# Three unused tiles that shift the operands of TensorE to multiples of 128 bytes

## The chip, the cores and the metric

One NeuronCore of a Trainium2 chip runs the whole program. The metric is the device time of one execution in microseconds, lower is better. The time before is the median of three executions.

## What is computed

A two-layer encoder trunk on one sequence of 1024 tokens with 1024 channels, all in float32. Cut to what matters here:

```python
for i in range(2):
    hdn = modulate(rmsnorm(x, mix_norm_g[i]), shift, scale)
    if i == 0:   # conv branch (width 31) beside a gMLP branch, one output projection
        y = conv_gmlp_mixer(hdn, ...)
    else:        # 8 heads, two softmax maps per head, relative position bias
        y = diff_attention(hdn, ...)
    x = x + gate * y
    hdn = modulate(rmsnorm(x, mlp_norm_g[i]), shift, scale)
    x = x + gate * (square(relu(hdn @ mlp_w1[i])) @ mlp_w2[i])   # 1024 -> 4096 -> 1024
return rmsnorm(x, final_norm_g)
```

## The kernel before

Activations lie transposed, channels on the 128 partitions and tokens along the free dimension, as tiles of 128 x 512 (`C = 512`, two column halves). Each float32 product is made as three matmuls in the `float32r` type (`mm3`, L124 to L128): both operands are split into a high part and the rest (`split`, L254 to L256: ScalarE casts the high part, VectorE subtracts), and high x high, high x low and low x high are summed in one bank of PSUM. In each, the weights (`whi`, `wlo`, 128 x 128) are the operand that is loaded into the array, and the activation (128 x 512) is the moving one. Weights come from memory as 128 x 1024 float32 (`raw`).

The stages in order: the first norm, the input projections, the convolution on VectorE (20 taps, L596), ScalarE and GpSimd, the gating and the output projection (to about 376 us); the first MLP (to about 1010 us); attention (to about 1690 us); the second MLP (to the end). The mixer's and the projections' moving operands are `hh`, `hl`, `zh`, `zl`, `th`, `tl`, `oh`, `ol` in pool `hp`; attention reads `K` (moving) with `Q` as weights (L957, L958), turns the softmax output `L` with transposes (L983) and reads `AT` (moving) with `Vh`, `Vl` as weights (L994 to L996).

`mlp` (L660) runs 8 groups of 7 steps. A step is one block product of a scheme of seven products with sums and differences of blocks (`UP`, `DOWN`, L656). It takes 48 matmuls: two halves of weights (`left`, L682) by four pieces of activation (`right`, L698) by two outputs by three. The activation pieces are tiles `b` of 128 x 2 x 512, high part and rest side by side, eight buffers. They are made one step ahead, or fetched from memory where an earlier group has already made them. Results leave PSUM by ScalarE and VectorE (`up_done`, L730; `down_done`, L741: VectorE L744). The modulation vectors of later layers are computed on VectorE in the background (L143).

Tiles are allocated in pools. Pools on the left side lie one behind the other from the low addresses up, those opened with `side="right"` from the top down; a pool takes the place of one that was closed before. The size of each tile is rounded up to 32 bytes. Addresses below are bytes within each partition. A 128 x 512 float32 tile takes 2048 bytes of each partition.

| tiles | pool, side | first address before | remainder to 128 | to 512 |
|---|---|---|---|---|
| `raw` (not the MLP's), `whi`, `wlo` | wp, left | 3968, 16256, 28544 | 0 | 384 |
| `h` tiles (`hh`, `hl`, `zh`, `zl`, `th`, `tl`, `f`) | hp, left | 40832 | 0 | 384 |
| `sq`, `ss`, `ht`, `ln`, `r` | tmp, left | 106368 | 0 | 384 |
| scalars of softmax and norm | small, left | 126848 | 0 | 384 |
| `b` (MLP); `K`, `V` (attention); `a0`, `a1` (conv) | mlp, at, mix, left | 127808 | 64 | 320 |
| `Q`; `raw` of the MLP | at, mlp, left | 160576 | 64 | 320 |
| `L`, `AT` | atr, right | 196576, 212960 | 96 | 480 |
| `x` | xp, right | 184288 | 96 | 480 |

`const` begins at 1152; its last tiles are `eps_r` (3840), `eps_l` (3872), `nlam` and `subg`. `wp`, `hp`, `tmp` and `small` follow it, and the pools of the stages (mix, mlp, at) begin where `small` ends, at 127808. The right side ends at 229344. The left pool `at` ends at 181056 and the right pool `atr` begins at 181216, 160 bytes above.

```python
    one = tmp.tile([P, P], F32, name="one", tag="sq", bufs=2)          # L73
    eps_r = const.tile([P, 1], F32, name="eps_r")                      # L77
    eps_l = const.tile([P, 1], F32, name="eps_l")                      # L78
```

## Time and profile before

| | |
|---|---|
| time, median of 3 (lowest to highest) | 2344.11 us (2333.05 to 2344.76) |
| the profiled execution's own time | 2343.52 us |
| its span, first to last instruction | 2341.7 us |
| granted TensorE clock, mean of the run | 0.984 of full |
| TensorE, VectorE, ScalarE, GpSimd busy | 2220.4, 1870.4, 1180.0, 238.2 us |
| matmuls | 10144 |

All instruction times are from the profiled execution. Matmuls are pipelined: the next one starts before the one in front is shown as ended, so the pace of a dense run is the difference of start times divided by the number of steps between them, not the duration of one.

### The profile page before, as it was taken

To read this page: it belongs to the slowest core of one execution; us is meant where nothing else is said; L and a number is where in the kernel's file an instruction comes from. 1 tells how busy PE (TensorE), PEld (TensorE's weight loads), DVE (VectorE), ACT (ScalarE), POOL (GpSimd) and SP (SyncE) were. 2 spreads that over 40 slices of the span, in tenths; PEclk is the share of its full clock that TensorE was granted. 3 is DMA by queue.
4 is the path that set the end of the run, shared out by engine and by line. 5 is a ranking of instruction groups with operands and counts; after the bars stand their busy time and mean duration, and the time that the engine had idled before them with its cause. 6 is when DMAs were issued, how large, how long until landed. Compare 5 with 4: busy or idle time off the path is not lost. (4 is left out here: it accounts for less than half of the span.)

```text
span 2341.7 us, 27508 instructions
## 1 busy us (share of the span) xinstructions
PE 2220.4 (95%) x10144; PEld 1798.3 (77%) x10144; DVE 1870.4 (80%) x2582; ACT 1180.0 (50%) x1753; POOL 238.2 (10%) x126
## 2 busy tenths in 40 slices
PE   4997599999999999979999999999999999999998
PEld 3786387778888888858888888887778888888886
DVE  8899899996785976986878888885798658577487
ACT  4563247633534535455656666653465354353455
POOL 0484000000000000031111111111000000000002
PEclk9998799999999999999999999999999999999999
DMA  8221553847457266233445333361362451633612
GB/s 315 84 79 45 197 183 115 305 128 276 153 178 277 86 220 245 86 110 96 86 97 107 75 83 71 86 193 60 132 238 83 162 207 54 219 123 116 237 43 73
DMA packets 113863, 335.17 MB, mean 143 GB/s; under 512 B 20576, under 2 KB 23520, under 8 KB 112704
## 3 DMA queue, kind: packets, MB, share of 16 engines
q1 hardware_dynamic: 113728, 333.41, 43.9%
q8 instruction: 80, 1.31, 0.2%
q14 instruction: 55, 0.45, 0.1%
HBM read 279.79 MB, written 53.58 MB: 142 GB/s over the span
## 5 line engine op out<-in xcount | busy, mean ns | idle before, releaser
L127 PE MATMUL ps<-b,whi 128*128 128x512 f32 (+1 forms) x1808 | 710.9, 394 | 6.5 <-DVE b L256 6.5
L126 PE MATMUL ps<-b,whi 128*128 128x512 f32 (+1 forms) x1808 | 702.2, 395 | 4.8 <-ACT b L255 3.0
L128 PE MATMUL ps<-b,wlo 128*128 128x512 f32 (+1 forms) x1808 | 703.2, 394 | 0.8 <-DVE wlo L256 0.8
L255 ACT CAST whi<-raw 128x1024 fp32r<-128x1024 f32 (+1 forms) x225 | 235.7, 1047 | 374.3 <-PE ps L127 336.9
L127 PEld LDWEIGHTS ps<-b,whi 128*128 128x128 f32 x1808 | 340.3, 188 | 90.6 <-DVE b L256 9.9
L126 PEld LDWEIGHTS ps<-b,whi 128*128 128x128 f32 x1808 | 340.0, 188 | 87.7 <-ACT b L255 3.9
L128 PEld LDWEIGHTS ps<-b,wlo 128*128 128x128 f32 x1808 | 340.1, 188 | 81.9 <-DVE wlo L256 1.6
L256 DVE TENSOR_TENSOR wlo<-raw,whi 128x1024 fp32r<-128x1024 f32 x224 | 273.3, 1220 | 146.0 <-ACT whi L255 144.0
L126 PE MATMUL ps<-hh,whi 128*128 128x512 f32 x576 | 225.4, 404 | 40.7 <-ACT hh L250 23.5
L127 PE MATMUL ps<-hl,whi 128*128 128x512 f32 x576 | 229.7, 399 | 4.3 <-DVE hl L251 2.9
L128 PE MATMUL ps<-hh,wlo 128*128 128x512 f32 x576 | 227.6, 396 | 0.0
L109 POOL TENSOR_TENSOR wlo<-raw,whi 128x1024 fp32r<-128x1024 f32 x32 | 83.5, 2612 | 1205.1 <-ACT whi L108 1044.0
L744 DVE SCALAR_TENSOR_TENSOR x<-ps,mod,x 128x512 f32<-128x512 f32 x220 | 160.3, 746 | 53.3 <-PE ps L128 53.3
L963 ACT ACTIVATE L<-L,mn 128x1024 f32<-128x1024 f32 x128 | 147.1, 1150 | 90.1 <-DVE mn L961 88.8
L961 DVE CUSTOM_DVE_ANT_0 L<-S,B 128x1024 f32<-128x1024 f32 x128 | 155.9, 1223 | 37.3 <-PE pt L983 18.4
L126 PEld LDWEIGHTS ps<-hh,whi 128*128 128x128 f32 x576 | 109.7, 191 | 68.8 <-ACT hh L250 27.7
L255 ACT CAST b<-f 128x512 fp32r<-128x512 f32 x192 | 118.0, 618 | 83.7 <-PE ps L128 83.3
L256 DVE TENSOR_TENSOR b<-f,b 128x512 fp32r<-128x512 f32 x192 | 128.9, 684 | 14.2 <-ACT b L255 14.2
L127 PEld LDWEIGHTS ps<-hl,whi 128*128 128x128 f32 x576 | 110.5, 192 | 29.4 <-DVE hl L251 5.5
L128 PEld LDWEIGHTS ps<-hh,wlo 128*128 128x128 f32 x576 | 110.5, 192 | 24.4 <-issue 0.5
L143 DVE CUSTOM_DVE_ANT_0 mraw<-mraw,cact 128x1024 f32<-128x1024 f32 x96 | 116.2, 1217 | 6.4 <-DMA mraw<-in_modw 6.3
L733 ACT COPY f<-ps 128x512 f32<-128x512 f32 x96 | 56.1, 588 | 128.4 <-PE ps L128 128.4
(201 smaller groups left out, 3473.9 us busy)
## 6 DMA issues: line engine op xcount, KB each, us to landing
b<-tspl SPq DMA_DIRECT2D x168, 512.0 KB, 5.2
raw<-in_wm SPq DMA_DIRECT2D x128, 512.0 KB, 4.6
mraw<-in_modw SPq DMA_DIRECT2D x96, 512.0 KB, 4.6
tspl<-b SPq DMA_DIRECT2D x56, 512.0 KB, 4.7
raw<-in_wqkv SPq DMA_DIRECT2D x24, 512.0 KB, 4.9
raw<-in_wo SPq DMA_DIRECT2D x17, 512.0 KB, 3.6
x<-in_xT SPq DMA_DIRECT2D x32, 256.0 KB, 5.8
tsr<-tsp SPq DMA_DIRECT2D x8, 1024.0 KB, 7.5
```

The lines of the kernel that those rows point to most:

```text
L109: (eng or dve).tensor_tensor(out=lo, in0=raw, in1=f32(hi), op=ALU.subtract)
L126: pe.matmul(ps, wh, ah, start=first, stop=False, skip_group_check=resumed)
L127: pe.matmul(ps, wh, al, start=False, stop=False, skip_group_check=resumed)
L128: newest[0] = pe.matmul(ps, wl, ah, start=False, stop=last, skip_group_check=resumed)
L143: i = dve.tensor_tensor_reduce(out=raw, in0=raw, in1=cact, op0=ALU.mult, op1=ALU.add, scale=1.0, scalar=0.0, accum_out=acc)
L255: act.copy(out=out_h, in_=src)
L256: (lo_eng or dve).tensor_tensor(out=out_l, in0=src, in1=f32(out_h), op=ALU.subtract)
L733: act.copy(out={"X1": c11, "Y1": c22, "X2": c12}[p], in_=ps)
L744: dve.scalar_tensor_tensor(out=x[m][c], in0=ps, scalar=gate(d, m), in1=x[m][c], op0=ALU.mult, op1=ALU.add)
L961: dve.tensor_tensor_reduce(out=L, in0=S, in1=win, op0=ALU.add, op1=ALU.min, scale=1.0, scalar=3e38, accum_out=mn)
L963: act.activation(out=L, in_=L, func=AF.Exp, bias=mn, scale=-1.0, accum_out=s[:, j:j + 1])
```

## The change

Three tiles are allocated that no instruction reads or writes, and the two constants of the norms share one tile of two columns.

```diff
     ones_r = const.tile([P, P], F32R, name="ones_r")
+
+    const.tile([P, 8], F32, name="fill")
+    small.tile([P, 16], F32, name="fills", tag="fills", bufs=1)
+    ctx.enter_context(tc.tile_pool(name="fillr", bufs=1, side="right")).tile([P, 24], F32, name="fillr")
     one = tmp.tile([P, P], F32, name="one", tag="sq", bufs=2)
...
-    eps_r = const.tile([P, 1], F32, name="eps_r")
-    eps_l = const.tile([P, 1], F32, name="eps_l")
+    eps = const.tile([P, 2], F32, name="eps")
+    eps_r, eps_l = eps[:, 0:1], eps[:, 1:2]
     pool.memset(eps_r, RMS_EPS)
     pool.memset(eps_l, LN_EPS)
```

By the sizes: `const` gains 32 bytes (`fill`) and loses 32 (two tiles of 4 bytes took 64, one of 8 takes 32), so `wp`, `hp` and `tmp` stay where they are. `small` grows by 64 bytes, so the left pools of the stages begin at 127872, which is 999 x 128 (remainder to 512: 384). `fillr` takes 96 bytes at the top of the right side, so all right tiles move down by 96; the side then ends at 229248, which is 1791 x 128 (remainder to 512: 384). `at` ends at 181120, and `atr` begins there. The scalar tiles in `small` move by 64 bytes.

## Rows read from the trace of the kernel before

**Rows 1.** Page: totals by engine; VectorE busy and granted clock in 40 slices.

```profile
PE 2220.4 (95%) x10144; PEld 1798.3 (77%) x10144; DVE 1870.4 (80%) x2582; ACT 1180.0 (50%) x1753; POOL 238.2 (10%) x126
...
DVE  8899899996785976986878888885798658577487
...
PEclk9998799999999999999999999999999999999999
```

**Rows 2.** Stretches: length, busy (count) by engine, clock, DMA share, GB/s; last two TensorE alone.

```profile
110.00:150.00 40.00, 40.00 (x178) 33.14 (x177) 38.90 (x32) 22.69 (x23) 29.86 (x12) 1.00 0.24 73
302.00:330.00 28.00, 28.00 (x125) 23.20 (x124) 28.00 (x48) 11.91 (x15) 0.00 (x0) 1.00 0.54 169
...
520.00:1010.00 490.00, 490.00 (x2102) 1.00 0.54 188
...
1740.00:2300.00 560.00, 560.00 (x2402) 1.00 0.41 141
```

**Rows 3.** Timeline of TensorE in the first MLP: start, length, line, operation, tiles.

```profile
599.71 0.40 PE L126 MATMUL ps<-b,whi 128*128 128x512 f32 x1
...
601.58 0.40 PE L128 MATMUL ps<-b,wlo 128*128 128x512 f32 x1
```

**Rows 4.** Timeline of TensorE in two projections of the mixer, ends of eight steps each.

```profile
119.74 0.39 PE L128 MATMUL ps<-hh,wlo 128*128 128x512 f32 x1
...
121.55 0.39 PE L127 MATMUL ps<-hl,whi 128*128 128x512 f32 x1
...
319.84 0.39 PE L128 MATMUL ps<-zh,wlo 128*128 128x512 f32 x1
...
321.65 0.39 PE L127 MATMUL ps<-zl,whi 128*128 128x512 f32 x1
```

**Rows 5.** Timeline of TensorE in attention: seven steps, four steps, transposes, 21 steps.

```profile
1105.18 0.39 PE L128 MATMUL ps<-hh,wlo 128*128 128x512 f32 x1
...
1106.77 0.39 PE L126 MATMUL ps<-hh,whi 128*128 128x512 f32 x1
...
1229.79 0.40 PE L958 MATMUL S<-K,Q 128*128 128x512 f32 x1
...
1230.71 0.40 PE L958 MATMUL S<-K,Q 128*128 128x512 f32 x1
1230.95 1.03 PE L983 MATMUL pt<-ident,L 128*128 128x128 f32 x8
...
1239.83 0.28 PE L996 MATMUL ps<-AT,Vl 128*128 128x256 f32 x1
...
1242.32 0.29 PE L996 MATMUL ps<-AT,Vl 128*128 128x256 f32 x1
```

**Rows 6.** Groups by shape, one of three lines: busy, mean ns, idle before, releasers.

```profile
L127 PE MATMUL ps<-b,whi 128*128 128x512 f32 x1776 | 701.8, 396 | 6.5 <-DVE b L256 6.5
```

**Rows 7.** The convolution's tap line: least/median/most ns, first and last start.

```profile
L596 DVE SCALAR_TENSOR_TENSOR ca<-ap,vec,ca x76: 1251/1290/1292, 86.1 to 267.7; 128x1024 f32<-128x1024 f32 x76
```

**Rows 8.** Stretches as in rows 2 before 520 us; TensorE's longest waits, 340 to 520.

```profile
400.00:430.00 30.00, 25.93 (x108) 19.43 (x107) 30.00 (x42) 18.60 (x31) 0.00 (x0) 1.00 0.66 230
...
495.00:520.00 25.00, 24.92 (x107) 20.13 (x108) 25.00 (x38) 9.64 (x14) 0.00 (x0) 1.00 0.49 151
...
PE ps L127 <- DVE b L256: 3.1, 2, 1.6
```

**Rows 9.** Timeline: VectorE reads a bank, TensorE writes the next product into it.

```profile
540.88 0.75 DVE L744 SCALAR_TENSOR_TENSOR x<-ps,mod,x 128x512 f32<-128x512 f32 x1
...
544.41 0.63 PE L126 MATMUL ps<-b,whi 128*128 128x512 f32 x2
```

**Rows 10.** TensorE's waits, whole run: total us, times, longest us.

```profile
PE ps L608 <- DVE a L597: 23.3, 1, 23.3
```

**Rows 11.** GpSimd's timeline at the start; first reader of the constants, first and last start.

```profile
0.91 0.10 POOL L80 MEMSET eps_l<- 128x1 f32 x1
...
L203 ACT ACTIVATE ln<-ps,eps_r x9: 687/687/689, 16.7 to 2312.7; 128x512 f32<-128x512 f32 x9
```

## The prediction

> **What bounds the kernel now.** I read the page's totals first, then busy time by stretch, then the timeline of single matmuls. TensorE is busy for 95% of the span at a granted clock of 0.984 over the run, and only the two slices from 176 to 293 us stand under nine tenths of full clock [rows 1]. Two stretches carry the case, one in each MLP: 520 to 1010 us and 1740 to 2300 us. In both TensorE has no gap at all, 490.00 of 490.00 and 560.00 of 560.00 us, and full clock [rows 2]. So there the time is the number of matmuls times their pace, and the question is the pace. A duration column doesn't give it, because matmuls overlap: each is shown as 0.39 us long while a new one starts every 0.23 us. The pace is the difference of starts.

> With `b` as moving operand (64 bytes past a multiple of 128), eight starts lie 601.58 - 599.71 = 1.87 us apart, 233.8 ns each [rows 3]. The long stretch agrees: 2102 matmuls touch 490.00 us, about two of them cut by its edges, so 490.00/2100 = 233.3 ns [rows 2]. I use 233.4. With operands at a multiple of 128 the same arithmetic gives 121.55 - 119.74 = 1.81 us for eight, 226.3 ns (`hh`, `hl`); 321.65 - 319.84, again 226.3 ns (`zh`, `zl`) [rows 4]; and 1106.77 - 1105.18 = 1.59 us for seven, 227.1 ns (`hh`, `hl` beside attention) [rows 5]. I use 226.7. The difference is 6.7 ns, 2.9% of a matmul.

> Is it the address, or the stage? Three things speak for the address. In attention `K`, at 64 past, takes 1230.71 - 1229.79 = 0.92 us for four, 230.0 ns, where the aligned `hh` of the same stage takes 227.1 [rows 5]. The aligned pace held while VectorE was busy for 38.90 and GpSimd for 29.86 of 40 us (40/176 = 227 ns), and, at 302 to 330 us, with VectorE never idle and DMA at 0.54, the share of the first MLP stretch (28/123 = 228 ns) [rows 2]. And the weights `whi`, `wlo` are at multiples of 128 in both cases, so the moving operand is what differs.

> **The change, part by part.** It removes and adds no matmul, copy or DMA; it moves addresses. After it `b`, `K`, `Q`, `V`, `AT`, `E`, `x` start at multiples of 128, and even the remainder to 512 becomes 384, the one that `h`, `whi` and `wlo` have now.

> (1) `b` in the gapless stretches. 1776 matmuls of 512 columns on each of three lines make 5328 [rows 6]; 2102 + 2402, less four at the edges, say 4500, are in the two stretches [rows 2]. 4500 x 6.7 ns = 30.2 us. This gain is kept only if the operands are ready 2.9% sooner. The tightest cover that I found there is a bank: VectorE ends its read at 540.88 + 0.75 = 541.63 us and TensorE writes into it again at 544.41 [rows 9], 2.8 us of slack; a step of 48 matmuls shrinks by 48 x 6.7 ns = 0.3 us. So VectorE isn't late next, unless it falls behind over some nine steps on end.

> (2) `b` before 520 us. From 400 to 430 us VectorE is busy for 30.00 of 30 us and TensorE for 25.93; TensorE waits for `b` [rows 8]. What a matmul gives up there is waited for. After 495 us TensorE is nearly gapless, 107 matmuls [rows 8]: 107 x 6.7 ns = 0.7 us. The bounds are 0 and the whole start of the MLP, 5328 - 4500 less about 220 after 1690 us, some 600 matmuls or 4.0 us; VectorE's full load puts the value near the lower end. The start of the second MLP, 1690 to 1740, has the same form: 0, at most 1.2 us.

> (3) The end, 2300 to 2342 us: some 30 whole `b`, 30 x 6.7 ns = 0.2 us, and the 96 of 256 columns of the last step, 0 to 0.5 us by the bounds of part (4). I take 0.6; bounds 0.2 and 0.7.

> (4) Attention. `K` as moving operand: 64 blocks, two maps, four matmuls each, 512 x (230.0 - 227.1) = 1.5 us. `AT` (96 past, 256 columns): 32 pairs of blocks of 24, pace (1242.32 - 1239.83)/21 = 118.6 ns [rows 5]. No aligned 256-column matmul is in the trace. Bounds: no gain, 118.6, since a weight load of 128 columns goes with each; and half of 226.7, 113.4, which is still above the pace of the transposes with the same weight load, 0.76/7 = 109 ns [rows 5]. That is 0 to 768 x 5.2 = 4.0 us. I take the middle, 2.0, as neither row is nearer. Counts are from the code (eight heads, eight blocks of queries). Softmax has its own chain over VectorE and ScalarE between two uses of TensorE, which may eat part of this, so of 3.5 us I count 3; bounds 0 and 5.5.

> (5) VectorE, ScalarE and DMA at new addresses: 0. The convolution's 76 tap instructions read the same tile at 20 offsets, 4 bytes apart, and take 1251/1290/1292 ns at least, median and most [rows 7]: no price by address. If this cover were gone, one part in a hundred of VectorE's 1870 us would be 19 us, but mostly beside TensorE.

> (6) One `eps` tile for two: the memsets stay. If readers of the first half now wait for both, they wait until 1.01 us [rows 11], while the first reader on ScalarE starts at 16.7 us [rows 11] and TensorE's sum of squares comes before it. 0. The three fillers have no instructions.

> Sum: 30.2 + 0.7 + 0 + 0.6 + 3 = 34.5 us. The profiled execution took 2343.5 us (span 2341.7 and 1.8 around it), 0.6 under the median of three, 2344.1. 2343.5 - 34.5 = 2309.0 us; against the median 2309.6. I predict 2309.

> [...] The rows show 233.4 against 226.7 ns for operands whose addresses are all multiples of 32 bytes [rows 3, 4]. [...]

> **The rivals.** A: the address costs nothing, and the 6.7 ns belong to something else of the `b` stages (two halves in one tile, the order of the banks), or the addresses don't come out as meant. Then nothing changes: 2344 us. For it: no `b` at a multiple of 128 is in the trace. Against it: `K` and `hh` in one stage. B: the pace falls, but VectorE, busy for five to nine tenths in the slices of the first gapless stretch [rows 1], becomes the bound in bursts and half of part (1) is waited for: 2309 + 15 = 2324 us. Against it: 2.8 us of slack at the tightest place. C, the other side: in 376 to 520 us TensorE's waits for VectorE grow, and the clock falls to its half level. There are about 600 `b` before 520 us; 600 x 227 ns more is 136 us, and 2309 + 136 = 2445 us. It decides when a pause is as long as those beside the low slices: TensorE waited 23.3 us for the convolution [rows 10], while the longest wait for `b` from 340 to 520 us is 1.6 us [rows 8]. Part (2) adds at most 4 us over many waits, so this is far off.

> **How the numbers follow.** Forecast 0.80, A 0.12, B 0.06, C 0.02. The low end takes all upper bounds: 30.2 + 4.0 + 1.2 + 0.7 + 5.5 = 41.6, 2302; the runs before reach 11 us under their median, and I allow 7 of it: 2295. The high end takes in B and some scatter: 2328. A measurement of this kernel tells about 0.5% (12 us) from no change, so faster is everything under 2332: forecast and B, 0.86; same is A, 0.12; slower is C, 0.02.

> **What would show it.** In the profile after: 520 to 1000 us should hold about 227 ns a `b`, so some 2115 instead of 2058 in 480 us; `K` should go to 227 ns; TensorE's gaps before 500 us should grow by 2 to 4 us; the taps should stay at 1290 ns. I'm wrong if `b` stays at 233 ns (A), if gaps appear in the two stretches (B), or if PEclk falls before 520 us (C).

## The result and the profile after

| | before | after |
|---|---|---|
| time, median | 2344.44 us (6 runs) | 2315.12 us (6 runs, 2312.81 to 2317.42) |
| ratio, 95% interval | 1 | 0.9882 [0.9862, 0.9901] |
| the profiled execution's own time | 2343.52 us | 2312.99 us |
| its span | 2341.7 us | 2311.2 us |

The kernel is 1.2% faster, 29 us by the medians. The forecast was 2309, with 2295 to 2328 as range. Four lines come in ahead of L73, so every line number behind them is four higher (L127 is L131).

The page after, totals by engine, granted clock in 40 slices, and the second of the three product lines (busy, mean ns of one | idle before it, releaser):

```profile
PE 2188.4 (95%) x10144; PEld 1800.3 (78%) x10144; DVE 1867.0 (81%) x2582; ACT 1180.8 (51%) x1753; POOL 238.5 (10%) x126
...
PEclk9998799999999999989999999999999999999999
...
L131 PE MATMUL ps<-b,whi 128*128 128x512 f32 (+1 forms) x1808 | 701.4, 389 | 6.7 <-DVE b L260 6.7
```

The same instructions run. TensorE is busy 32 us less than in [rows 1], and every other engine as long as it was. The idle time ahead of the `b` products is 6.7 us, where [rows 6] has 6.5: the gain was not turned into waits.

Stretches after, columns as in rows 2; the last two are from the view of TensorE alone:

```profile
400.00:430.00 30.00, 26.37 (x107) 20.27 (x106) 30.00 (x42) 18.50 (x30) 0.00 (x0) 0.94 0.65 228
495.00:520.00 25.00, 25.00 (x111) 20.70 (x111) 25.00 (x37) 10.36 (x15) 0.00 (x0) 1.00 0.49 151
...
520.00:1000.00 480.00, 480.00 (x2116) 1.00 0.56 194
1740.00:2280.00 540.00, 540.00 (x2396) 1.00 0.40 136
```

The MLP stretches are still without a gap, and hold more matmuls: 2116 touch the first, where 2115 were forecast. The timeline of TensorE after, 12 steps apart:

```profile
599.17 0.39 PE L130 MATMUL ps<-b,whi 128*128 128x512 f32 x1
...
601.89 0.39 PE L130 MATMUL ps<-b,whi 128*128 128x512 f32 x1
```

2.72/12 = 226.7 ns, where [rows 3] gives 233.8. From 400 to 430 us VectorE is still busy for all 30 us and the count of matmuls is the old one [rows 8].

Attention after, timeline of TensorE: three steps of `K`, then 21 of `AT`:

```profile
1237.08 0.39 PE L962 MATMUL S<-K,Q 128*128 128x512 f32 x1
...
1237.77 0.29 PE L999 MATMUL ps<-AT,Vh 128*128 128x256 f32 x1
1237.90 0.28 PE L1000 MATMUL ps<-AT,Vl 128*128 128x256 f32 x1
...
1240.41 0.28 PE L1000 MATMUL ps<-AT,Vl 128*128 128x256 f32 x1
```

`K` takes (1237.77 - 1237.08)/3 = 230 ns, as in [rows 5], though it now lies at a multiple of 128. `AT` takes 2.51/21 = 119.5 ns, more than the 118.6 of [rows 5]. These are single groups. Over all groups of `K`, the steps behind the first of a group take 231.2 ns on average before and 230.0 after (two of over 300 ns left out in each); over all 32 runs of 21 steps `AT` takes 118.2 and 119.8. `K` got 1.2 ns of the 2.9 that were forecast and `AT` went the other way: the first sign that "a multiple of 128" is not what counts.

TensorE's matmuls stand in the same order in both traces, so the start of the n-th (counted from 0) can be compared. The gain so far, by stage:

| matmul | start before | after less before | gained in the stage |
|---|---|---|---|
| 1800th (first MLP, still led by VectorE) | 511.5 us | -0.74 us | 0.74 |
| 3900th (first MLP, no gaps) | 1001.5 | -14.74 | 14.00 = 2100 x 6.67 ns |
| 4200th (pause, start of attention) | 1091.4 | -16.63 | 1.89 |
| 7200th (end of attention) | 1644.9 | -16.20 | -0.43 |
| 7500th (start of the second MLP) | 1723.0 | -14.97 | -1.23 |
| 9900th (second MLP) | 2283.8 | -30.64 | 15.67 = 2400 x 6.53 ns |
| last | 2331.4 | -30.76 | 0.12 |

The changed kernel was run once more later (after_again). Its trace has 0.30, 14.00, 0.30, -0.29, -0.33, 15.68 and 0.60 us in the last column, against the same trace of before. So the two stretches without gaps repeat, while the other stages differ by up to 1.6 us between two executions of one kernel.

### The profile page after: what moved, and what is told of

Its sections match the earlier page's. It is cut to its first block, busy times and chain, and to the rows that moved or that the text cites. A ratio compares the mean times of both kernels' runs of the same rounds, so it can differ in the third digit from the quotient of the medians.

```text
span 2311.2 us, 27508 instructions
## 1 busy us (share of the span) xinstructions
PE 2188.4 (95%) x10144; PEld 1800.3 (78%) x10144; DVE 1867.0 (81%) x2582; ACT 1180.8 (51%) x1753; POOL 238.5 (10%) x126
## 5 line engine op out<-in xcount | busy, mean ns | idle before, releaser
L131 PE MATMUL ps<-b,whi 128*128 128x512 f32 (+1 forms) x1808 | 701.4, 389 | 6.7 <-DVE b L260 6.7
L130 PE MATMUL ps<-b,whi 128*128 128x512 f32 (+1 forms) x1808 | 692.8, 390 | 5.1 <-ACT b L259 4.6
L132 PE MATMUL ps<-b,wlo 128*128 128x512 f32 (+1 forms) x1808 | 693.6, 388 | 1.9 <-DVE wlo L260 1.9
L131 PEld LDWEIGHTS ps<-b,whi 128*128 128x128 f32 x1808 | 340.7, 188 | 79.7 <-DVE b L260 9.5
L131 PE MATMUL ps<-hl,whi 128*128 128x512 f32 x576 | 229.4, 399 | 4.1 <-DVE hl L255 2.6
L131 PEld LDWEIGHTS ps<-hl,whi 128*128 128x128 f32 x576 | 110.5, 192 | 29.3 <-DVE hl L255 5.5
```

The source lines that it names most:

```text
L130: pe.matmul(ps, wh, ah, start=first, stop=False, skip_group_check=resumed)
L131: pe.matmul(ps, wh, al, start=False, stop=False, skip_group_check=resumed)
L132: newest[0] = pe.matmul(ps, wl, ah, start=False, stop=last, skip_group_check=resumed)
```

## The experiments

In what follows the *distance* is the start of the moving operand less the start of the weights, in bytes within a partition, as remainder to 256. Before, `b` lay at distance 192 (64 less 128), `hh` at 0, `K` at 0 from `Q`, `AT` at 160 from `V`. After the change all are at 0.

**b_at_0: only `b` and the MLP's `raw` move.** A pad of 64 bytes at the head of the MLP's pool; nothing else changes.

```diff
+            mp.tile([P, 16], F32, name="pad")
             f = [[hp.tile([P, C], F32, name="f", tag="h", bufs=32) for c in range(NC)] for m in range(KT)]
```

> The kernel before with one unused tile of 64 bytes at the head of the MLPs' pool: only b (and the MLPs' raw weights, which TensorE doesn't read) moves from 64 past a multiple of 128 to a multiple; K, Q, V, AT, L and x stay where they were. Theory (the address of the moving operand b sets the pace, nothing else in the change matters): b at 227 ns in 540 to 980 us, 4500 x 6.7 ns = 30 us, so 2344 - 31 = 2313 us, the same as the whole change within its scatter. Rival (the gain comes from x, L, AT or K, or from the scalars that moved): near 2344 us.

2314.75 us, ratio 0.9876 [0.9862, 0.9889], the same as the whole change. The stretch 520 to 980 us of this kernel (length, TensorE busy and count, clock, DMA share, GB/s):

```profile
520.00:980.00 460.00, 460.00 (x2031) 1.00 0.57 197
```

460.00/2029 = 226.7 ns. All that can be measured of the change's gain comes from `b`.

**b_at_32 and b_at_96: `b` at 32 and at 96 past a multiple of 128** (pads of 24 and 8 floats, distances 32 and 224).

```diff
+            mp.tile([P, 24], F32, name="pad")    # b_at_96: [P, 8]
```

> The same with an unused tile of 96 bytes, so that b lies 32 bytes past a multiple of 128. Theory 1 (every start that isn't a multiple of 128 costs the same, since one more piece of 128 bytes is touched): 233.4 ns a matmul, 2344 us as before. Theory 2 (the price grows with the bytes past the multiple): about 230 ns, 2344 - 15 = 2329 us. Rival (128 isn't the unit, 32 is enough): 227 ns, 2313 us.

> The same with an unused tile of 32 bytes, so that b lies 96 bytes past a multiple of 128. Theory 1 (one price for every start off a multiple): 233.4 ns, 2344 us. Theory 2 (the price grows with the bytes past the multiple): about 237 ns, 5328 x 3.3 ns = 15 to 18 us more than before, 2360 us. Rival (32 is enough): 227 ns, 2313 us.

2344.35 and 2344.46 us, ratios 1.0001 [0.9991, 1.0010] and 1.0001 [0.9992, 1.0010]. The same stretch of b_at_32 (b_at_96 has the same count):

```profile
520.00:980.00 460.00, 460.00 (x1973) 1.00 0.56 193
```

460.00/1971 = 233.4 ns at 32 and 96 past, as at 64 past before. The price doesn't grow with the remainder.

**attn_only: only attention's tiles move.** `K`, `V`, `Q` and `AT` come to multiples of 128, and `AT` to distance 0 from `V`; `b` stays.

```diff
     ap = ast.enter_context(opened(name="at", bufs=1))
+    ap.tile([P, 16], F32, name="pad")
...
         atr = ctx.enter_context(ExitStack())
+        atr.enter_context(opened(name="padr", bufs=1, side="right")).tile([P, 24], F32, name="padr")
```

> The kernel before with an unused tile of 64 bytes in attention's left pool and one of 96 bytes above its right pool: K, Q, V, AT, L and the bias window move to multiples of 128, b and x stay where they were. In the profile after the change, K fell from about 232 to 230 ns and AT rose from 118 to 120 ns, and attention was no shorter. Theory (the two cancel): 2344 us, within 0.2%. Rival (attention gains its 3 us, and something else of the change took it back): 2341 us, and attention 3 us shorter by its profile.

2344.68 us, ratio 1.0000 [0.9991, 1.0009]. Its timeline of TensorE, 21 steps of `AT`:

```profile
1241.62 0.28 PE L997 MATMUL ps<-AT,Vl 128*128 128x256 f32 x1
...
1244.14 0.28 PE L997 MATMUL ps<-AT,Vl 128*128 128x256 f32 x1
```

2.52/21 = 120.0 ns; the mean of all 32 runs is 119.7, where before has 118.2. `K` takes 230.2 ns inside its groups, where before has 231.2: 512 x 1.0 = 0.5 us against 768 x 1.5 = 1.2 us the other way. Between its 4200th and 7200th matmul attention is as long as before, to 0.01 us. So the change does nothing useful here, and `AT` is slower at distance 0 than at 160.

**no_const_fill: all left tiles at 96 past a multiple of 128, together.** The changed kernel without the filler in `const`: weights, `h` tiles and `b` all move down by 32, their distance stays 0. `AT` comes to distance 32 from `V`.

```diff
-    const.tile([P, 8], F32, name="fill")
```

> The changed kernel without its first filler (32 bytes in the constants' pool): everything behind the constants on the left side moves down by 32, so that weights, h tiles, b, K, Q and V all lie 96 past a multiple of 128; AT, L and x stay at multiples. Theory (the moving operand's start sets the pace of every 512-column matmul): b, hh, hl, zh, zl, th, tl all at the pace that b_at_96 shows; with 233 ns about 1 to 2 us per 200 dense matmuls, 2344 us plus up to 2000 x 6.7 = 13 us for the other operands, less what waits for VectorE, 2350 us. Rival (the MLP's b alone is sensitive): 2344 us with hh and zh still at 227 ns.

2312.45 us, ratio 0.9863 [0.9847, 0.9880]. The stretch 520 to 980 us, and 21 steps of `AT` in the timeline:

```profile
520.00:980.00 460.00, 460.00 (x2031) 1.00 0.57 197
...
1237.58 0.28 PE L999 MATMUL ps<-AT,Vl 128*128 128x256 f32 x1
...
1240.03 0.28 PE L999 MATMUL ps<-AT,Vl 128*128 128x256 f32 x1
```

`b` takes 226.7 ns although no left tile is at a multiple of 128. That refutes the rule of the prediction: the address by itself is not it. Neither of the two expected times, 2350 and 2344 us, came. `AT` takes 2.45/21 = 116.7 ns.

**paces: dense runs with the trunk left out.** 48 matmuls of one kind on end, with the weights stepping by 128 columns and the moving operand by 512 (512 and 2048 bytes, so the distance stays the same), both starts chosen.

```python
for r in range(48):
    a, b = m // 4 + 512 * (r % 6), w // 4 + 128 * (r % 12)
    pe.matmul(ps[:, 0:n], wts[:, b:b + P], mov[:, a:a + n], start=r == 0, stop=r == 47)
```

> Only dense runs of 48 matmuls in float32r on TensorE, nothing beside them, the trunk left out: the moving operand starts m bytes and the weights w bytes past a multiple of 128, with 512, 384, 256 or 128 columns. Theory (address of the moving operand alone): 512 columns at 226.7 ns for m = 0, 128 and 192-64, that is 227 at m = 0 and 128, 233 at m = 64 and 192, whatever w is. Theory 1: every other m costs as much as 64. Theory 2: the price grows with m. Rival A (the pace belonged to the MLP stage): 227 ns for all m. At 256 columns, from the profile after the change: 120 ns at m = 0, 118 at m = 64 and 96, that is the aligned start is the slower one; if it was the weights' address that did it, then 120 only for w = 0.

The pace is the difference of a run's start and the next one's, by 48; a name gives columns, moving operand `m` and weights `w`, in bytes past the first address of their tiles, which both have remainder 384 to 512. Four rows of its timeline (start, length, line, operation):

```profile
79.72 11.20 PE L72 MATMUL n512m48w0x<-mov,wts 128*128 128x512 f32 x48
90.76 11.17 PE L72 MATMUL n512m64w0x<-mov,wts 128*128 128x512 f32 x48
...
224.80 5.82 PE L72 MATMUL n256m0w64x<-mov,wts 128*128 128x256 f32 x48
230.45 5.92 PE L72 MATMUL n256m64w64x<-mov,wts 128*128 128x256 f32 x48
```

Each dense kernel was executed once. With 512 columns `m` at 0 takes 226.7 ns, at 64 229.2, at 128 232.4 and at 192 233.2, and with the weights at 64 `m` at 0 takes 233.3 and at 64 227.3. So the pace doesn't belong to the MLP (rival A), nor does it follow the moving operand's start alone. The one start off a multiple of 16, `m` at 4, is the slowest, 236.2 ns. Three cases show no dependence: 384 columns (173.9 and 173.2 ns at `m` 0 and 64), 128 columns (110.6 to 111.7 at three layouts) and plain float32 (429.1 and 429.2).

**paces_fine: the same, every 16 bytes to 256, every 32 to 480, and with several starts of the weights.**

> Dense runs of 48 matmuls alone again, the trunk left out, moving operand m bytes and weights w bytes past the first address, both tiles at the same remainder to 512. Theory R (the distance m - w, to 256 bytes): 226.7 ns at m = 0 and 256; equal pace for equal distance: (192, 128) and (256, 192), (128, 64) as (64, 0), 229 ns; (160, 128) as (32, 0), 233.3; (64, 192) and (0, 128) as (128, 0), 232.4; m from 256 to 480 repeats m from 0 to 224. Theory of the prediction (the address of the moving operand, to 128): all of m = 0, 128, 256, 384 at 226.7, and (192, 128) and (64, 192) off it. If the period is 512: m = 256 is slow. For 256 columns: 120 ns at distance 0, 113.5 at 112, and (160, 64), (176, 64) as (96, 0), (112, 0).

The timeline of paces_fine: start, length, line, operation; names as in paces.

```profile
35.21 11.04 PE L72 MATMUL n512m0w0x<-mov,wts 128*128 128x512 f32 x48
46.09 11.28 PE L72 MATMUL n512m16w0x<-mov,wts 128*128 128x512 f32 x48
57.21 11.37 PE L72 MATMUL n512m32w0x<-mov,wts 128*128 128x512 f32 x48
68.41 11.36 PE L72 MATMUL n512m48w0x<-mov,wts 128*128 128x512 f32 x48
79.60 11.16 PE L72 MATMUL n512m64w0x<-mov,wts 128*128 128x512 f32 x48
90.60 11.25 PE L72 MATMUL n512m80w0x<-mov,wts 128*128 128x512 f32 x48
...
123.99 11.32 PE L72 MATMUL n512m128w0x<-mov,wts 128*128 128x512 f32 x48
135.15 11.36 PE L72 MATMUL n512m144w0x<-mov,wts 128*128 128x512 f32 x48
...
168.79 11.35 PE L72 MATMUL n512m192w0x<-mov,wts 128*128 128x512 f32 x48
179.98 11.42 PE L72 MATMUL n512m208w0x<-mov,wts 128*128 128x512 f32 x48
...
202.44 11.05 PE L72 MATMUL n512m240w0x<-mov,wts 128*128 128x512 f32 x48
213.32 11.08 PE L72 MATMUL n512m256w0x<-mov,wts 128*128 128x512 f32 x48
224.24 11.37 PE L72 MATMUL n512m288w0x<-mov,wts 128*128 128x512 f32 x48
235.45 11.16 PE L72 MATMUL n512m320w0x<-mov,wts 128*128 128x512 f32 x48
246.44 11.37 PE L72 MATMUL n512m352w0x<-mov,wts 128*128 128x512 f32 x48
...
324.49 11.15 PE L72 MATMUL n512m128w64x<-mov,wts 128*128 128x512 f32 x48
335.48 11.35 PE L72 MATMUL n512m160w128x<-mov,wts 128*128 128x512 f32 x48
...
357.82 11.30 PE L72 MATMUL n512m0w128x<-mov,wts 128*128 128x512 f32 x48
368.96 5.92 PE L72 MATMUL n256m0w0x<-mov,wts 128*128 128x256 f32 x48
374.71 5.87 PE L72 MATMUL n256m16w0x<-mov,wts 128*128 128x256 f32 x48
380.42 5.76 PE L72 MATMUL n256m32w0x<-mov,wts 128*128 128x256 f32 x48
386.02 5.84 PE L72 MATMUL n256m48w0x<-mov,wts 128*128 128x256 f32 x48
...
437.04 5.62 PE L72 MATMUL n256m192w0x<-mov,wts 128*128 128x256 f32 x48
442.50 5.88 PE L72 MATMUL n256m208w0x<-mov,wts 128*128 128x256 f32 x48
```

With 512 columns, distance 0 takes (46.09 - 35.21)/48 = 226.7 ns, 16 takes 231.7, 32 takes 233.3, 64 takes 229.2, 128 takes 232.5 and 192 takes 233.1. The first and the last of these are the two paces of the kernel, with nothing else running. Distance 240, not tried in the kernel, is as fast as 0: (213.32 - 202.44)/48 = 226.7. Weights at 64 and the moving operand at 128 give 10.99/48 = 229.0, as 64 and 0; weights at 128 and the moving operand at 0 give 11.14/48 = 232.1, as distance 128; and a moving operand at 256 or 320 takes 227.5 or 229.0, as one at 0 or 64. So the difference of the starts counts, and which of the two is "aligned" doesn't. With 256 columns distance 0 takes 5.75/48 = 119.8 ns, 32 takes 116.7 and 192 takes 113.8: there 0 is the worst of these, and the same order stands in attention (119.5 at 0; 118.6 at 160, before; 116.7 at 32).

The distance doesn't fix the pace in every case. At distance 48, with the same addresses, 512 columns take (79.60 - 68.41)/48 = 233.1 ns here and (90.76 - 79.72)/48 = 230.0 in paces. At distance 192, 256 columns take 113.8 here (192 and 0) and (230.45 - 224.80)/48 = 117.7 in paces (0 and 64).

**b_at_128: at a multiple of 128, but at distance 128.** This separates the two rules in the whole kernel.

```diff
+            mp.tile([P, 48], F32, name="pad")
```

> The kernel before with an unused tile of 192 bytes at the head of the MLPs' pool: b now starts at a multiple of 128 (remainder to 256: 0), while the weights keep theirs (remainder to 256: 128). Theory of the prediction (a moving operand at a multiple of 128 takes 226.7 ns): 2313 us, as b_at_0. Theory R, formed from the run without the first filler (all operands 96 past, yet fast) and from the dense runs: what counts is the distance between moving operand and weights, to 256 bytes; distance 128 took 232.4 ns in the dense runs, so 4500 x 1 ns less than before, 2340 us.

2340.79 us, ratio 0.9983 [0.9968, 0.9998]. The stretch 520 to 980 us:

```profile
520.00:980.00 460.00, 460.00 (x1981) 1.00 0.55 193
```

460.00/1979 = 232.4 ns, the dense run's value for distance 128. A `b` that lies at a multiple of 128 bytes, as the change asks, is worth about 4 us, not 30.

**best and after_again: a layout made by distances, beside the changed kernel.** `b` at 0 from its weights, `AT` at 192 from `V`; two pairs of constants share tiles to make the room.

```diff
-    eps_r = const.tile([P, 1], F32, name="eps_r")
-    eps_l = const.tile([P, 1], F32, name="eps_l")
+    eps = const.tile([P, 2], F32, name="eps")
+    eps_r, eps_l = eps[:, 0:1], eps[:, 1:2]
...
-        nlam = const.tile([P, 1], F32, name="nlam")
+        lamg = const.tile([P, 2], F32, name="lamg")
+        nlam, subg = lamg[:, 0:1], lamg[:, 1:2]
...
-        subg = const.tile([P, 1], F32, name="subg")
...
+            mp.tile([P, 16], F32, name="pad")
...
+        atr.enter_context(opened(name="padr", bufs=1, side="right")).tile([P, 8], F32, name="padr")
```

> Another layout, made by the distances (start of the moving operand less start of the weights, to 256 bytes): b and whi/wlo at distance 0, as in b_at_0; AT and Vh/Vl at 192, where the dense runs had 113.3 ns for 256 columns (160 in the kernel before, 0 in the changed kernel). Two pairs of one-column constants share a tile each, which makes the room; the sources of all other left tiles move by 64 bytes together. Theory (the distance alone sets the pace): b 226.8 ns, AT 113.4 ns; the gain of b_at_0 (29.7 us) and 768 x (118.5 - 113.4) = 3.9 us in attention, of which softmax may eat half: 2311 to 2313 us, ratio 0.986. If the pace of AT is not on the path of attention (softmax sets it): AT 113.4 ns, but 2314.8 us as b_at_0. If the dense runs say nothing of AT in its place: AT stays at 117 to 120 ns and 2314.8 us.

> The changed kernel once more, beside the layout made by distances on the same chip. Theory and rivals alike: 2315.1 us, ratio 0.988; AT at distance 0 takes 119.8 to 120 ns.

2311.65 us, ratio 0.9857 [0.9841, 0.9874], against 2314.16 us, 0.9864 [0.9844, 0.9883]. The intervals overlap: that best is the faster one isn't shown. Two runs of 21 steps of `AT` in its timeline:

```profile
1206.30 0.28 PE L997 MATMUL ps<-AT,Vl 128*128 128x256 f32 x1
...
1208.77 0.28 PE L997 MATMUL ps<-AT,Vl 128*128 128x256 f32 x1
...
1241.05 0.28 PE L997 MATMUL ps<-AT,Vl 128*128 128x256 f32 x1
...
1243.43 0.28 PE L997 MATMUL ps<-AT,Vl 128*128 128x256 f32 x1
```

The first takes 2.47/21 = 117.6 ns, the second 2.38/21 = 113.3. Of the 32 such runs 12 take 113.3 to 114.3 ns and 20 take 117.8; the mean is 116.3. Each keeps its pace from its first few steps to its end. So the dense run's 113.8 was only one of two paces at this distance. Both had been seen before: paces has 117.7, which the expectation left out, and the 256-column products of `b` before, also at distance 192, take 117.8. The expected 3.9 us became 768 x (118.2 - 116.3) = 1.5 us; the trace has attention 1.3 us shorter than before. That fits, but b_at_128, whose attention lies as before, has it 2.0 us longer, so one trace doesn't show it. What decides between the two paces at the start of a run is open.

## Why the prediction held, and where it didn't

**The view that carried it** was right: two stretches without gaps, the time there is count times pace, and the pace is the difference of starts. Term (1), 30.2 us for 4500 matmuls, measured 14.00 + 15.67 = 29.7 us. No gap came up (rival B is out), so the 2.8 us of slack [rows 9] was enough.

**The step that failed** is the one behind "Is it the address, or the stage?". The prediction took the remainder of the moving operand to 128 for the cause, noted that the weights lie at multiples of 128 "in both cases", and dropped them. They are half of the cause: distance 192 takes 233.1 ns and distance 0 takes 226.7 in the dense runs; no_const_fill keeps the pace with nothing aligned, and b_at_128 loses nearly all of it with `b` aligned. That the forecast came out is luck in this respect: the change happens to bring `b` to distance 0 as well. The control that was to prove the address, `K` at 230.0 against `hh` at 227.1 [rows 5], proved nothing: `K` and `Q` were at distance 0 before and after, and `K` still takes 230. Its mean goes with the layout at one and the same distance: 231.2 ns at 64 past a multiple of 128 (before, b_at_0), 230.0 to 230.2 at a multiple of 128 (after, attn_only), 229.6 at 96 past (no_const_fill). So for groups this short neither rule is the whole one. What holds `K` near 230 ns was not tried.

**Term (4)**, attention, gave none of its 3 us (bounds 0 and 5.5): attention is 0.43 us longer in this trace, 0.29 in after_again, and unchanged in attn_only. A loss isn't shown, since b_at_0, whose attention lies as before, has 0.37. `K` gave 512 x 1.2 = 0.6 us of its 1.5. `AT` was to gain 2.0; its sign was wrong, by 119.8 against 118.2 ns, 768 x 1.6 = 1.2 us. The bound "no gain, 118.6" at the lower end was no bound.

**Term (2)** agrees, 0.7 forecast and 0.74 measured, but after_again has 0.30, b_at_0 0.29 and best a loss of 1.05, so one trace can't carry it. What else the shorter matmuls gave up was waited for, with VectorE busy all the time from 400 to 430 us: TensorE is busy for 171.18 us between 340 and 520 us where it was for 172.65, 1.5 us more idle, less than the 2 to 4 that were forecast. The start of the second MLP, forecast at 0 to 1.2 of gain, lost 1.23. There TensorE pauses, for 2.70 and 1.10 us in both traces, and its granted clock behind the pause is 0.50. The granted clock in stretches of 2 us, after:

```profile
1676.00:1678.00 2.00, 2.00 (x5) 0.50 0.62 250
1678.00:1680.00 2.00, 2.00 (x7) 0.50 0.99 404
1680.00:1682.00 2.00, 2.00 (x6) 0.53 0.77 309
```

and before, where the rise came sooner behind the same pause:

```profile
1692.00:1694.00 2.00, 1.82 (x4) 0.50 0.52 213
1694.00:1696.00 2.00, 2.00 (x8) 0.72 0.99 406
```

At a granted clock of 0.50 to 0.53, 5 to 7 matmuls touch a stretch of 2 us, where 9 and 10 do at 1.00 (the two from 1682 to 1686 us, after). b_at_0 loses 0.1 us between the same two matmuls, no_const_fill gains 0.4 and best loses 1.0, so this is scatter of one execution and no price of the change. The 1.89 us gained in the pause ahead of attention is of the same kind: b_at_0 loses 1.0 there, no_const_fill gains 1.8. **Term (3)**, forecast at 0.6, gave 0.12 here and 0.60 in after_again; its 96 matmuls of 256 columns got slower, 119.7 ns where they took 117.8 before, 0.2 us. **Terms (5) and (6)** held: VectorE, ScalarE and GpSimd are as busy as before, and the taps take the same, as their row after shows (least/median/most ns):

```profile
L600 DVE SCALAR_TENSOR_TENSOR ca<-ap,vec,ca x76: 1251/1290/1290, 86.5 to 268.0; 128x1024 f32<-128x1024 f32 x76
```

**The sum.** 34.5 us forecast, 30.5 us between the two profiled executions. The 4.0 us are 3.4 of attention, 0.5 of the pace, 1.2 of the second MLP's start and 0.5 of the end, less the 1.9 ahead of attention; the 0.3 that are left lie behind the last matmul. Of these only the pace and attention's missing gain repeat in after_again. The profiled execution after lies 2.1 us under its median, which makes the 6 us between 2309 and 2315.1.

**The rivals.** A said that the address costs nothing and something else of the `b` stages does: wrong, since b_at_0 moves the addresses alone and has the whole gain, but its doubt about the cause was sound. C, the clock, showed in small. One stretch after, TensorE alone:

```profile
405.00:410.00 5.00, 4.50 (x15) 0.66 0.49 198
```

The wait for `b` just before grew from 1.56 to 1.93 us, and the clock fell to 0.50 for part of these 5 us (0.50 from 406 to 408 us, 0.66 over the five; 0.54 in after_again, 1.00 before). The longer wait alone doesn't decide it: b_at_0, no_const_fill and best wait 1.91 to 1.92 us there and keep 1.00. It cost nothing that can be seen, with VectorE busy throughout this stage: the 1800th matmul starts 0.74 us sooner all the same.

## What to carry to other kernels

When TensorE runs without gaps, compare the difference of starts between stages with the same shape; 3% between them (233.4 against 226.7 ns here) is worth finding. Then look at both operands: in these runs the pace of long `float32r` runs went with the distance between the moving tile and its weights, and an unused tile of 64 bytes in one pool changes it (b_at_0, 226.7 ns where 233.4 stood). Measure it for the width and in the place in use, since the best distance for 512 columns (0, 226.7 ns) was among the worst for 256 (119.8 ns, where distance 192 has 113.8 or 117.7). And ask what else the fast cases share: here every fast operand was both at a multiple of 128 and at distance 0 from its weights, so the trace of before couldn't tell the two apart, and one unused tile (b_at_128) could.
